# Shifted weight tiles for products of halves, and four leading tiles by ordinary products, in a two-layer hybrid network on Trainium2

## The chip, the cores and the metric

The kernel runs on one core of one Trainium2 chip. The metric is the device time of one execution in microseconds (us). The kernel before has a median of 2090.86 us over three runs (2090.5 to 2095.24). Engines go by short names: PE is TensorE, DVE VectorE, ACT ScalarE, POOL GpSimd, SP the engine that issues most DMAs.

## The reference, cut to what matters

Two layers run over a sequence of 512 tokens of width 1024. Each layer is a feed-forward block (FFN), a mixer block of three parallel mixers, and a second FFN. The change sits in the FFNs:

```python
def rmsnorm(x, g, eps=NORM_EPS):
    y = xf * lax.rsqrt(jnp.mean(xf * xf, axis=-1, keepdims=True) + eps)
    return y * g.astype(jnp.float32)

def swiglu(h, wg, wu, wd):
    return (jax.nn.silu(h @ wg) * (h @ wu)) @ wd

for i in range(DEPTH):                      # DEPTH = 2
    h = rmsnorm(x, ffn1_norm[i])
    x = x + MACARON_WEIGHT * swiglu(h, ffn1_wg[i], ffn1_wu[i], ffn1_wd[i])
    ...                                     # mixers
    h = rmsnorm(x, ffn2_norm[i])
    x = x + MACARON_WEIGHT * swiglu(h, ffn2_wg[i], ffn2_wu[i], ffn2_wd[i])
```

`wg` and `wu` are 1024 x 2816 (22 column tiles of 128), `wd` is 2816 x 1024. All is float32.

## The kernel before, in words

**Layout.** Activations lie transposed: 8 tiles of 128 channels x 512 tokens. Each float32 product is made of three products of a faster type (`float32r`): every operand is split into a high part (ACT copies it, rounded) and a low part (DVE subtracts), and PE adds high x high, high x low and low x high in a PSUM bank. Weights come from DRAM into `raw` (3 buffers), and their two parts go to `whi` and `wlo` (3 buffers each). `places()` allots all large tiles first, so that each starts at a multiple of 512 bytes.

**Ordinary products.** `gemm` (lines 269 to 287) makes a 128 x 512 output tile from 8 channel tiles: 3 x 8 = 24 matmuls of 512 columns, at lines 277, 285 and 286. `load_w` fetches and splits one weight tile (lines 262 and 263). `single` multiplies a gate tile and an up tile by the norm's factor (lines 521 and 522), applies silu, multiplies and splits the result.

**Products of halves.** Three of the four FFNs go through `ffn_halves`: the second of layer 0, and both of layer 1. It takes the 22 tile columns of `wg` and `wu` in pairs. For a pair `halves` makes, instead of 8 block products, 7 products of blocks of half the size (a scheme of Strassen and Winograd): `product` (lines 426 to 439) issues for each of them 3 x 4 = 12 matmuls of 256 columns at lines 436, 437 and 438, so one call of `halves` has 84 and one pair of tile columns, gate and up, has 168. Sums and differences of weight blocks are made by DVE (lines 462, 464, 479, 481) in `QG` and `ES`, and split like other weights (`split`, lines 290 and 291). Sums and differences of the activations, `T1` to `T4`, are made once for each FFN by `halves_of` (lines 407 to 423), four calls, each with two multiplications on ACT (line 415), three subtractions on DVE (419 to 421) and a split (290, 291) into `b0`, `b1`, `b2`, `b4`, `b5`, `b6` and `x`.

**Order.** `norm` first splits the 8 activation tiles without the norm's factor and lets PE begin at once; the factor `rstd` follows and is multiplied in when a PSUM bank is emptied. `gate(0)` makes the tile columns 0 and 1 by ordinary products (`firsts`: three weight tiles side by side in the three `mm` banks, the fourth in an `ms` bank) and then calls `halves_of`. `gate(1)` to `gate(10)` are pairs by halves. The down products (`down`, ordinary, into `ms` banks) come in groups behind the gates. A scheduler orders the instructions of each engine from the program's order and its own estimates; `behind` adds ordering constraints.

Of the kernel before, what the change touches and what calls it, by code (L numbers as in the profile page):

```python
# [8 lines left out]
F32 = mybir.dt.float32  # L9
F32R = mybir.dt.float32r  # L10
I32 = mybir.dt.int32
# [8 lines left out]
KD = D // 128  # L20
# [6 lines left out]

TAGS = {
    "x": (1024, 4), "hh": (512, 8), "hl": (512, 8),
    "raw": (1024, 3), "whi": (1024, 3), "wlo": (1024, 3),  # L30
    "rstd": (512, 1), "gain": (32, 2),
# [5 lines left out]
}  # L37
ORDER = ("x", "hh", "hl", "bk", "qr", "bh", "whi", "wlo", "b0", "b1", "b2", "b3", "b4", "b5", "b6", "QG", "ES", "yf",
         "bon", "g", "raw", "tm", "sg", "kk", "sq", "y", "w", "rstd", "kr")

# [68 lines left out]
def layout(z):  # L109
# [41 lines left out]
    def tiles(w):  # L151
# [3 lines left out]
    zz, xbc, dt, s, r = np.split(z["w_in"], [512, 1536, 1544, 1800], axis=2)  # L155
    t = lambda a, j: a[:, :, 128 * j:128 * j + 128]
    w_in = np.concatenate([s, t(r, 6), t(r, 2), t(r, 0), t(r, 4), t(r, 3), t(r, 1), t(r, 5)]
                          + [q for g in range(2) for q in (xbc[:, :, 256 * g:256 * g + 256], t(xbc, 4 + g),
                                                           t(xbc, 6 + g), zz[:, :, 256 * g:256 * g + 256])], 2)
    out = {  # L160
        "cst": constants(),
# [14 lines left out]
class Kernel:  # L176
# [5 lines left out]
    def places(self):  # L182

        start = self.sb.tile([128, 96], F32, tag="start", name="start", bufs=1)
        for tag in ORDER:
            n, bufs = TAGS[tag]
            assert n % 128 == 0
            self.sb.tile([128, n], F32, tag=tag, name=tag, bufs=bufs)

    def t(self, tag, shape, dt=F32):  # L190
        n, bufs = TAGS[tag]
        v = self.sb.tile([128, n], dt, tag=tag, name=tag, bufs=bufs)
        f = 1
        for s in shape[1:]:
            f *= s
        assert f <= n, (tag, shape)
        v = v[0:shape[0], 0:f]
        if len(shape) == 3:
            v = v.rearrange("p (a b) -> p a b", b=shape[2])
        elif len(shape) == 4:  # L200
            v = v.rearrange("p (a b c) -> p a b c", b=shape[2], c=shape[3])
        return v
# [238 lines left out]
    def halves(self, w, ops, out, n):  # L441

        nc = self.nc
        V = nc.vector
        H = L // 2
        raw = [self.fetch_w(w[m], KD, 128, [slice(0, KD)]) for m in range(2)]
        quarter = lambda m, k: raw[m].rearrange("p (q o) c -> p q o c", o=2)[:, :, k]
        hl = lambda shape: [self.t(t, shape, F32R) for t in ("whi", "wlo")]
        at = lambda w, o: [(lambda q, a=a: a[:, o, q]) for a in w]
        f = lambda a: a.rearrange("p s q c -> p (s q) c")  # L450
        snap = self.t(("bon", "g")[n % 2], [128, 4, H])
        keep = lambda j, r, by=1.0: nc.scalar.activation(out=snap[:, j], in_=r, func=AF.Copy, scale=by)

        w1 = hl([128, KD, 128])
        self.behind(self.split(raw[0], *w1), self.normed)
        w1 = [a.rearrange("p (q o) c -> p o q c", o=2) for a in w1]
        r1 = self.bank("mm", H)
        self.product(r1, at(w1, 0), ops, "B11", last=False)
        keep(0, r1)

        S = self.t(("QG", "ES")[n % 2], [128, 16, 128]).rearrange("p (s q) c -> p s q c", s=4)
        s1 = V.tensor_tensor(out=S[:, 0], in0=quarter(1, 0), in1=quarter(1, 1), op=ADD)
        self.behind(s1, self.normed)
        V.tensor_tensor(out=S[:, 1], in0=S[:, 0], in1=quarter(0, 0), op=SUB)
        w2 = hl([128, KD, 128])
        self.split(f(S[:, 0:2]), *w2)
        w2 = [a.rearrange("p (o q) c -> p o q c", o=2) for a in w2]
        r2 = self.bank("mr", H)
        self.product(r2, at(w1, 1), ops, "B21")
        V.tensor_tensor(out=out[:, 0, 0:H], in0=r2, in1=snap[:, 0], op=ADD)  # L470
        r3 = self.bank("mm", H)
        self.product(r3, at(w2, 0), ops, "T1", last=False)
        keep(3, r3)
        self.product(r1, at(w2, 1), ops, "T2", first=False, last=False)
        keep(1, r1)

        w4 = hl([128, KD // 2, 128])
        self.split(quarter(1, 1), *w4)
        s3 = V.tensor_tensor(out=S[:, 2], in0=quarter(0, 0), in1=quarter(1, 0), op=SUB)
        self.behind(s3, self.normed)  # L480
        V.tensor_tensor(out=S[:, 3], in0=quarter(0, 1), in1=S[:, 1], op=SUB)
        w3 = hl([128, KD, 128])
        self.split(f(S[:, 2:4]), *w3)
        w3 = [a.rearrange("p (o q) c -> p o q c", o=2) for a in w3]
        r4 = self.bank("mr", H)
        self.product(r4, [(lambda q, a=a: a[:, q]) for a in w4], ops, "T4")
        keep(2, r4, -1.0)
        self.product(r3, at(w3, 1), ops, "B22", first=False)
        V.tensor_tensor(out=out[:, 0, H:L], in0=r3, in1=snap[:, 1], op=ADD)
        self.product(r1, at(w3, 0), ops, "T3", first=False)  # L490
        V.tensor_tensor(out=out[:, 1], in0=r1.unsqueeze(1).to_broadcast([128, 2, H]), in1=snap[:, 2:4], op=ADD)

    def ffn_halves(self, gain, f, i, end=False):
        nc = self.nc
        wg, wu, wd = (self.a[f"{f}_{w}"][i] for w in ("wg", "wu", "wd"))
        act, rstd = self.norm(gain)
        slots = [self.t(n, [128, 2, 2 * L], F32R) for n in ("bk", "qr", "bh")]
        wide = rstd.unsqueeze(1).to_broadcast([128, 2, L])
        ops = []
# [7 lines left out]
        def firsts():  # L507

            w = lambda a, j: self.load_w(a[j], KD, 128)
            three = [(self.bank("mm"), w(*q)) for q in ((wg, 0), (wu, 0), (wg, 1))]  # L510
            self.gemms(three, act)
            ps = self.bank("ms")
            rest = w(wu, 1)
            single(0, three[0][0], three[1][0])
            self.gemm(ps, rest, act)
            single(1, three[2][0], ps)
# [13 lines left out]
        def gate(p):  # L530
            if p == 0:
                firsts()
                ops.extend(self.halves_of(act, gain, q) for q in range(KD // 2))
                return
            s, u = (self.t("p", [128, 2, L]) for _ in range(2))
            self.halves(wg[2 * p:2 * p + 2], ops, s, 0)
            nc.vector.tensor_tensor(out=s, in0=s, in1=wide, op=MUL)
            nc.scalar.activation(out=s, in_=s, func=AF.Silu)
            self.halves(wu[2 * p:2 * p + 2], ops, u, 1)
            nc.vector.tensor_tensor(out=u, in0=u, in1=wide, op=MUL)  # L540
            nc.vector.tensor_tensor(out=u, in0=u, in1=s, op=MUL)
            g = slots[p % 3]
            self.split(u, g[:, :, 0:L], g[:, :, L:2 * L])
            gs.extend((g[:, j, 0:L], g[:, j, L:2 * L]) for j in range(2))

        gs, left = [], []
        for n, (k0, nk) in enumerate(PAIRED):
# [5 lines left out]
            if end and first is None:  # L553
                ws = [self.load_w(wd[m, :, k0:k0 + nk], nk, 128, q)
                      for m, q in enumerate(("b0", "b1", "b2", "b4", "b5", "b6", "bon", "g"))]
                for h in range(2):
                    t = slice(256 * h, 256 * h + 256)
# [858 lines left out]
    def s5_tables(self, i):  # L1416

        nc = self.nc
        V, G = nc.vector, nc.gpsimd
        sp = self.small("s5p", [128, 4, 16])  # L1420
        self.dma(out=sp, in_=self.a["s5p"][i].rearrange("p (n g) -> p n g", n=4))
        sm = self.t("sg", [128, L])
        nxt = [128]
# [1 line left out]
        def t():  # L1425
            o = nxt[0]
            nxt[0] += 16
            return sm[:, o:o + 16]
# [1 line left out]
        pw = (lambda a: (a[:, 0], a[:, 1]))(self.t("g", [128, 2, L]))  # L1430
        v9 = lambda j: pw[j // 3][:, 144 * (j % 3):144 * (j % 3) + 144].rearrange("p (d g) -> p d g", g=16)
        PR, PI, SR, SI, NI, NR = (v9(j) for j in range(6))
        up = self.small("s5r", [128, 2, 8, 16])
        RR, RI = up[:, 0], up[:, 1]
        m1, m2 = (sm[:, 64 * j:64 * j + 64].rearrange("p (d g) -> p d g", g=16) for j in range(2))
        are, aim, ldt = (sp[:, j] for j in range(3))
        dt, mag, th, kq, co, si, w, w2 = (t() for _ in range(8))
        e1, e2, e3 = (t() for _ in range(3))
        ei = self.small("s5i", [128, 16], I32)
        self.exp_exact(ldt, dt, e1, e2, e3, ei)  # L1440
        V.tensor_tensor(out=w, in0=are, in1=dt, op=MUL)
        self.exp_exact(w, mag, e1, e2, e3, ei)
# [149 lines left out]
        G.memset(dT[:, :, 0:1], 0.0)  # L1592
        G.tensor_copy(out=dT[:, :, 1:], in_=mag.unsqueeze(2).to_broadcast([128, 16, 63]))
        self.s5 = halves, cT, sT, dT
        if i:
            self.s5_away(6, cT, sT, dT)
# [11 lines left out]
    def s5_again(self):  # L1608

        cut = [q for n in ("QG", "ES") for q in (lambda a: (a[:, 0:8], a[:, 8:16]))(self.t(n, [128, 16, 128]))]  # L1610
        cut += [self.t(n, [128, 8, 128]) for n in ("b0", "b1")]
        v = lambda q: q.rearrange("p g (d h) -> p g d h", h=16)
        halves = [(cut[n], v(cut[n + 1]), v(cut[n + 2])) for n in (0, 3)]
        self.s5 = halves, *(self.t(q, [128, 16, 64]) for q in ("b4", "b5", "b6"))
        halves, *rest = self.s5
        for n, q in enumerate(self.s5_flat((*halves[0], *halves[1], *rest))):
            self.nc.gpsimd.dma_start(out=q, in_=self.s5d[n])
# [187 lines left out]
```

## Time and profile before

| what | value |
|---|---|
| median of three runs | 2090.86 us |
| the profiled execution | 2088.86 us |
| span of its instructions | 2087.1 us |
| PE busy | 2002.3 us (96%), 16008 matmuls |
| DVE busy | 1578.0 us (76%) |
| ACT busy | 916.5 us (44%) |
| POOL busy | 361.0 us (17%) |
| mean granted PE clock | 0.983 of full speed |
| DMA | 200 MB, mean 96 GB/s |

The span is the time from the first to the last instruction of the one execution that was profiled; 1.8 us lie around it. That execution is 2.0 us under the median. PE busy is a sum of intervals that overlap (matmuls are pipelined), so the distance from the start of one matmul to the start of the next is the better measure of what one costs. The granted clock is either full (2.4 GHz) or half (1.2 GHz); a mean between tells how long each was granted.

### The profile page before, as it was taken

To read this page: it belongs to the slowest core of one execution; us is meant where nothing else is said; L and a number is where in the kernel's file an instruction comes from. 1 tells how busy PE (TensorE), PEld (TensorE's weight loads), DVE (VectorE), ACT (ScalarE), POOL (GpSimd) and SP (SyncE) were. 2 spreads that over 40 slices of the span, in tenths; PEclk is the share of its full clock that TensorE was granted. 3 is DMA by queue.
4 is the path that set the end of the run, shared out by engine and by line. 5 is a ranking of instruction groups with operands and counts; after the bars stand their busy time and mean duration, and the time that the engine had idled before them with its cause. 6 is when DMAs were issued, how large, how long until landed. Compare 5 with 4: busy or idle time off the path is not lost.

```text
span 2087.1 us, 39669 instructions
## 1 busy us (share of the span) xinstructions
PE 2002.3 (96%) x16008; PEld 1716.1 (82%) x16008; DVE 1578.0 (76%) x2570; ACT 916.5 (44%) x1404; POOL 361.0 (17%) x715
## 2 busy tenths in 40 slices
PE   8999999998999899999989999999899998999997
PEld 6788888776777699999969999987677777999996
DVE  6546555597569988877798888777956798888886
ACT  4222323443443645444464444444434445444443
POOL 0867656014121000000000000000222200000002
PEclk9999999999999999999999999999999999999998
DMA  4334332331202233333223333354111232333332
GB/s 158 113 117 137 112 112 82 125 122 33 61 12 77 84 101 96 107 112 102 75 96 102 92 103 105 110 191 150 51 54 35 60 96 66 106 101 102 91 103 80
DMA packets 89750, 200.00 MB, mean 96 GB/s; under 512 B 19040, under 2 KB 31328, under 8 KB 89568
## 3 DMA queue, kind: packets, MB, share of 16 engines
q1 hardware_dynamic: 82240, 186.85, 28.7%
q0 software_dynamic: 2592, 9.44, 1.2%
q8 instruction: 126, 2.06, 0.4%
q10 hardware_dynamic: 4736, 1.18, 0.3%
q14 instruction: 56, 0.46, 0.1%
HBM read 184.19 MB, written 12.06 MB: 94 GB/s over the span
## 4 chain that ended last, share of the span: by engine, by line
PE 79%; DVE 11%; issue 3%; ACT 2%; DMA 2%; POOL 1%; ACTq 0%; SPq 0%; POOLq 0%; DVEq 0%
PE mm L277 9%; PE mm L285 8%; PE mm L286 8%; PE mm L436 7%; PE mm L438 7%; PE mm L437 7%; PE ms L286 6%; PE ms L277 6%; PE ms L285 5%; PE mr L437 3%; PE mr L436 3%; PE mr L438 3%; DVE wlo L263 2%; PE mr L1039 1%; DMA raw<-in_ffn_wu 1%
## 5 line engine op out<-in xcount | busy, mean ns | idle before, releaser
L262 ACT ACTIVATE whi<-raw 128x512 fp32r<-128x512 f32 (+3 forms) x333 | 238.4, 718 | 476.2 <-PE mm L285 216.3
L277 PE MATMUL mm<-hh,whi 128*128 128x512 f32 x864 | 353.3, 412 | 18.3 <-ACT whi L262 14.2
L285 PE MATMUL mm<-hl,whi 128*128 128x512 f32 x864 | 341.4, 395 | 1.4 <-DVE hl L291 1.4
L286 PE MATMUL mm<-hh,wlo 128*128 128x512 f32 x864 | 342.3, 397 | 0.5 <-DVE wlo L263 0.5
L263 DVE TENSOR_TENSOR wlo<-raw,whi 128x512 fp32r<-128x512 f32 (+3 forms) x333 | 281.8, 848 | 58.8 <-ACT whi L262 58.0
L277 PEld LDWEIGHTS mm<-hh,whi 128*128 128x128 f32 x864 | 164.7, 191 | 60.3 <-ACT whi L262 18.8
L286 PEld LDWEIGHTS mm<-hh,wlo 128*128 128x128 f32 x864 | 163.8, 190 | 37.9 <-DVE wlo L263 1.8
L285 PEld LDWEIGHTS mm<-hl,whi 128*128 128x128 f32 x864 | 164.5, 190 | 32.9 <-DVE hl L291 2.5
L436 PE MATMUL mm<-b,whi 128*128 128x256 f32 x540 | 155.5, 288 | 24.4 <-ACT whi L290 24.4
L290 ACT ACTIVATE whi<-raw 128x1024 fp32r<-128x1024 f32 x120 | 101.5, 846 | 173.2 <-PE mm L437 104.6
L437 PE MATMUL mm<-b,whi 128*128 128x256 f32 x540 | 154.8, 287 | 0.0
L438 PE MATMUL mm<-b,wlo 128*128 128x256 f32 x540 | 154.8, 287 | 0.0
L438 PE MATMUL mm<-hh,wlo 128*128 128x256 f32 x480 | 135.9, 283 | 0.6 <-DVE wlo L291 0.6
L437 PE MATMUL mm<-hl,whi 128*128 128x256 f32 x480 | 135.1, 283 | 0.0
L436 PE MATMUL mm<-hh,whi 128*128 128x256 f32 x480 | 135.1, 283 | 0.0
L436 PEld LDWEIGHTS mm<-b,whi 128*128 128x128 f32 x540 | 105.9, 196 | 25.0 <-ACT whi L290 25.0
L291 DVE TENSOR_TENSOR wlo<-raw,whi 128x1024 fp32r<-128x1024 f32 x120 | 114.3, 952 | 5.1 <-ACT whi L290 4.5
L437 PEld LDWEIGHTS mm<-b,whi 128*128 128x128 f32 x540 | 105.9, 196 | 0.0
L438 PEld LDWEIGHTS mm<-b,wlo 128*128 128x128 f32 x540 | 105.6, 196 | 0.0
L436 PEld LDWEIGHTS mm<-hh,whi 128*128 128x128 f32 x480 | 91.9, 192 | 1.6
L438 PEld LDWEIGHTS mm<-hh,wlo 128*128 128x128 f32 x480 | 92.0, 192 | 1.2 <-DVE wlo L291 0.8
L437 PEld LDWEIGHTS mm<-hl,whi 128*128 128x128 f32 x480 | 91.9, 191 | 1.2
(653 smaller groups left out, 5152.6 us busy)
## 6 DMA issues: line engine op xcount, KB each, us to landing
raw<-in_ffn_wu SPq DMA_DIRECT2D x88, 512.0 KB, 3.7
raw<-in_ffn_wg SPq DMA_DIRECT2D x87, 512.0 KB, 3.7
raw<-in_ffn_wd SPq DMA_DIRECT2D x152, 256.0 KB, 2.6
raw<-in_w_in SPq DMA_DIRECT2D x42, 512.0 KB, 3.7
raw<-in_w_out SPq DMA_DIRECT2D x32, 128.0 KB, 2.3
raw<-in_w_out SPq DMA_DIRECT2D x16, 256.0 KB, 2.7
raw<-in_ffn_wd SPq DMA_DIRECT2D x16, 192.0 KB, 2.4
xd<-x SPq DMA_DIRECT2D x12, 256.0 KB, 4.3
```

The lines of the kernel that those rows point to most:

```text
L262: nc.scalar.activation(out=hi[:, q], in_=raw[:, q], func=AF.Copy)
L263: sub = nc.vector.tensor_tensor(out=lo[:, q], in0=raw[:, q], in1=hi[:, q].bitcast(F32), op=SUB)
L277: first = nc.tensor.matmul(out=ps, lhsT=hi[:, k], rhs=ah, start=(k == 0), stop=False)
L285: nc.tensor.matmul(out=ps, lhsT=hi[:, k], rhs=al, start=False, stop=False)
L286: mm = nc.tensor.matmul(out=ps, lhsT=lo[:, k], rhs=ah, start=False, stop=(k == last))
L290: self.nc.scalar.activation(out=hi, in_=src, func=AF.Copy)
L291: return self.nc.vector.tensor_tensor(out=lo, in0=src, in1=hi.bitcast(F32), op=SUB)
L436: nc.tensor.matmul(out=ps, lhsT=hi(q), rhs=ah, start=first and q == 0, stop=False, skip_group_check=True)
L437: nc.tensor.matmul(out=ps, lhsT=hi(q), rhs=al, start=False, stop=False, skip_group_check=True)
L438: nc.tensor.matmul(out=ps, lhsT=lo(q), rhs=ah, start=False, stop=last and q == len(ops) - 1, skip_group_check=True)
L1039: nc.tensor.matmul(out=b[s, j], lhsT=lh[s, j], rhs=rh[s, j], start=True, stop=True)
```

## The change

Three things are edited. The two weight tiles get 128 more elements, and in `halves` their data start 16 elements (64 bytes) into the tile, while the moving operands stay at multiples of 512 bytes (`SHIFT`, and the argument `o` of `t`); `load_w` and so all ordinary products keep weights at multiples of 512 bytes. `gate(1)` makes the tile columns 2 and 3 by four ordinary products, and two calls of `halves_of` stand behind each of the two gate-and-up pairs; `gate(0)` no longer calls it. The small tables of the S5 mixer (`s5p`, `s5r`, `s5i`) lie in tile `b3` in place of tiles of their own.

```diff
-    "raw": (1024, 3), "whi": (1024, 3), "wlo": (1024, 3),
+    "raw": (1024, 3), "whi": (1152, 3), "wlo": (1152, 3),
...
+SHIFT = 16
...
-    def t(self, tag, shape, dt=F32):
+    def t(self, tag, shape, dt=F32, o=0):
...
-        assert f <= n, (tag, shape)
-        v = v[0:shape[0], 0:f]
+        assert o + f <= n, (tag, shape)
+        v = v[0:shape[0], o:o + f]
...
-        hl = lambda shape: [self.t(t, shape, F32R) for t in ("whi", "wlo")]
+        hl = lambda shape: [self.t(t, shape, F32R, SHIFT) for t in ("whi", "wlo")]
...
         def gate(p):
             if p == 0:
                 firsts()
-                ops.extend(self.halves_of(act, gain, q) for q in range(KD // 2))
+                return
+            if p == 1:
+
+                for j in (2, 3):
+                    w = [self.load_w(a[j], KD, 128) for a in (wg, wu)]
+                    ps = [self.bank("mm") for _ in w]
+                    for q in zip(ps, w):
+                        self.gemm(*q, act)
+                    ops.extend(self.halves_of(act, gain, q) for q in (2 * j - 4, 2 * j - 3))
+                    single(j, *ps)
                 return
...
-        sp = self.small("s5p", [128, 4, 16])
+        own = self.t("b3", [128, 512])
+        sp = own[:, 0:64].rearrange("p (n g) -> p n g", n=4)
...
-        up = self.small("s5r", [128, 2, 8, 16])
+        up = own[:, 64:320].rearrange("p (n d g) -> p n d g", n=2, d=8)
...
-        ei = self.small("s5i", [128, 16], I32)
+        ei = own[:, 320:336].bitcast(I32)
```

Lines move by 2 up to `halves` (the products are at 438 to 440, `gemm` at 279, 287 and 288, the splits at 292 and 293) and by 11 or 12 behind `gate`.

The rows below are from the second FFN of layer 0; the two FFNs of layer 1 have the same pattern.

**PE, from the last ordinary product to the products of halves.** Names with a number are buffers: `mm_7405` is the bank of the first product of halves, `mm_7440` the first that needs the second weight tile `whi_7422` and the activation sums `b0`, `b1`. Before:

```order
L436 MATMUL mm_7405<-hh_7162,whi_7401 128x256
L437 MATMUL mm_7405<-hl_7163,whi_7401 128x256
L438 MATMUL mm_7405<-hh_7162,wlo_7402 128x256
L436 MATMUL mm_7440<-b0_7360,whi_7422 128x256
L437 MATMUL mm_7440<-b1_7361,whi_7422 128x256
L436 MATMUL mm_7405<-b0_7360,whi_7422 128x256
L437 MATMUL mm_7405<-b1_7361,whi_7422 128x256
L436 MATMUL mr_7477<-b0_7360,whi_7467 128x256
```

And changed, where `mm_7453` is the bank of the up product of tile column 3, and `mm_7541` of the first product of halves:

```order
L279 MATMUL mm_7453<-hh_7164,whi_7448 128x512
L287 MATMUL mm_7453<-hl_7165,whi_7448 128x512
L288 MATMUL mm_7453<-hh_7164,wlo_7449 128x512
L438 MATMUL mm_7541<-hh_7125,whi_7537 128x256
L439 MATMUL mm_7541<-hl_7126,whi_7537 128x256
L440 MATMUL mm_7541<-hh_7125,wlo_7538 128x256
L438 MATMUL mm_7541<-hh_7136,whi_7537 128x256
L439 MATMUL mm_7541<-hl_7137,whi_7537 128x256
```

The 24 matmuls of 512 columns of each of `mm_7362`, `mm_7363`, `mm_7452` and `mm_7453` now stand ahead of the first product of halves, and the 168 matmuls of 256 columns of the pair of tile columns 2 and 3 are gone.

**DVE, behind the last write of the norm (`sg`).** `mm` in the last row is the bank of the gate product of tile column 0. Before:

```order
L337 TENSOR_TENSOR sg<-cst,rrmry 128x512
L291 TENSOR_TENSOR wlo<-raw,whi 128x1024
L419 TENSOR_TENSOR QG<-QG 128x512
L419 TENSOR_TENSOR ES<-ES 128x512
L420 TENSOR_TENSOR QG<-QG 128x256
L521 TENSOR_TENSOR sq<-mm,rstd 128x512
```

And changed:

```order
L339 TENSOR_TENSOR sg<-cst,rrmry 128x512
L265 TENSOR_TENSOR wlo<-raw,whi 128x1024 x2
L421 TENSOR_TENSOR QG<-QG 128x512
L421 TENSOR_TENSOR ES<-ES 128x512
L523 TENSOR_TENSOR sq<-mm,rstd 128x512
```

One more weight tile is subtracted ahead of the emptying of the first `mm` bank, and one half-size subtraction less.

**DVE, up to the low part of the second weight tile of the first pair by halves (`wlo<-QG`).** Before:

```order
L291 TENSOR_TENSOR b_7381<-QG,b_7380 128x1024
L470 TENSOR_TENSOR p<-mr,bon 128x256
L291 TENSOR_TENSOR bk<-w,bk 128x512
L291 TENSOR_TENSOR x<-ES,x 128x1024
L462 TENSOR_TENSOR QG<-raw 128x512
L479 TENSOR_TENSOR QG<-raw 128x512
L291 TENSOR_TENSOR bk<-y,bk 128x512
L464 TENSOR_TENSOR QG<-QG,raw 128x512
L481 TENSOR_TENSOR QG<-raw,QG 128x512
L291 TENSOR_TENSOR wlo<-QG,whi 128x1024
```

And changed:

```order
L265 TENSOR_TENSOR wlo<-raw,whi 128x1024
L464 TENSOR_TENSOR QG<-raw 128x512
L481 TENSOR_TENSOR QG<-raw 128x512
L293 TENSOR_TENSOR x<-ES,x 128x1024
L466 TENSOR_TENSOR QG<-QG,raw 128x512
L524 TENSOR_TENSOR w<-mm,rstd 128x512
L293 TENSOR_TENSOR wlo<-raw,whi 128x1024
L483 TENSOR_TENSOR QG<-raw,QG 128x512
L526 TENSOR_TENSOR w<-w,sq 128x512
L523 TENSOR_TENSOR kk<-mm,rstd 128x512
L293 TENSOR_TENSOR qr<-w,qr 128x512
L293 TENSOR_TENSOR wlo<-QG,whi 128x1024
```

The chain that ends in `wlo<-QG` now has the emptying of the banks of tile columns 2 and 3 and their weights between its parts.

## Rows read from the trace of the kernel before

**Rows 1.** The page's part 1: span, and busy us of each engine.

```profile
span 2087.1 us, 39669 instructions
...
PE 2002.3 (96%) x16008; PEld 1716.1 (82%) x16008; DVE 1578.0 (76%) x2570; ACT 916.5 (44%) x1404; POOL 361.0 (17%) x715
```

**Rows 2.** What PE waited for, whole span: us in total, times, longest us.

```profile
PE mm L436 <- ACT whi L290: 24.4, 3, 8.1
```

**Rows 3.** PE timeline at the first such wait: start us, us, engine, line, operation.

```profile
721.25 0.28 PE L438 MATMUL mm<-hh,wlo 128*128 128x256 f32 x1
...
729.65 0.58 PE L436 MATMUL mm<-b,whi 128*128 128x256 f32 x1 [8.13 <-ACT whi L290]
```

**Rows 4.** PE timeline behind the second such wait; 9 starts apart.

```profile
1090.13 0.41 PE L438 MATMUL mm<-b,wlo 128*128 128x256 f32 x1
...
1092.05 0.41 PE L438 MATMUL mm<-x,wlo 128*128 128x256 f32 x1
```

**Rows 5.** Busy us by stretch: PE, PEld, DVE, ACT, POOL, then granted clock, DMA.

```profile
729.60:734.60 5.00, 4.95 (x25) 4.95 (x26) 4.47 (x6) 1.85 (x3) 0.00 (x0) 0.55 0.65 204
1088.60:1093.60 5.00, 4.92 (x27) 4.92 (x28) 4.42 (x6) 1.89 (x4) 0.00 (x0) 0.61 0.60 204
1746.60:1751.60 5.00, 4.93 (x24) 4.93 (x25) 4.54 (x6) 1.87 (x4) 0.00 (x0) 0.53 0.67 206
```

**Rows 6.** PE timeline, the last ordinary product of tile column 1.

```profile
718.50 0.39 PE L286 MATMUL ms<-hh,wlo 128*128 128x512 f32 x1
```

**Rows 7.** DVE timeline behind the norm.

```profile
715.54 1.22 DVE L291 TENSOR_TENSOR wlo<-raw,whi 128x1024 fp32r<-128x1024 f32 x1
...
717.88 0.42 DVE L420 TENSOR_TENSOR QG<-QG 128x256 f32<-128x256 f32 x1
...
718.21 0.69 DVE L521 TENSOR_TENSOR sq<-mm,rstd 128x512 f32<-128x512 f32 x1
```

**Rows 8.** ACT and DVE timeline, second weight tile of the first pair by halves.

```profile
728.54 1.06 ACT L290 ACTIVATE whi<-QG 128x1024 fp32r<-128x1024 f32 x1 [4.39 <-DVE QG L464]
...
729.63 1.23 DVE L291 TENSOR_TENSOR wlo<-QG,whi 128x1024 fp32r<-128x1024 f32 x1 [0.40 <-ACT whi L290]
```

**Rows 9.** PE timeline, products of halves in full flow; 12 starts apart.

```profile
1950.25 0.28 PE L436 MATMUL mm<-hh,whi 128*128 128x256 f32 x1
...
1951.69 0.28 PE L438 MATMUL mm<-b,wlo 128*128 128x256 f32 x1
```

**Rows 10.** PE timeline, ordinary products in full flow; 4 starts apart.

```profile
914.07 0.39 PE L286 MATMUL ms<-qr,wlo 128*128 128x512 f32 x1
...
914.98 0.39 PE L277 MATMUL ms<-bh,whi 128*128 128x512 f32 x1
```

**Rows 11.** PE timeline, first products of halves behind ordinary ones; 3 starts apart.

```profile
768.18 0.28 PE L436 MATMUL mm<-hh,whi 128*128 128x256 f32 x1
...
768.52 0.28 PE L436 MATMUL mm<-hh,whi 128*128 128x256 f32 x1
```

**Rows 12.** PE timeline, first ordinary products behind halves; 4 starts apart.

```profile
788.68 0.40 PE L277 MATMUL ms<-bk,whi 128*128 128x512 f32 x1
...
789.61 0.39 PE L285 MATMUL ms<-bk,whi 128*128 128x512 f32 x1
```

**Rows 13.** Line 436, first and last of six rows: duration ns, starts, forms.

```profile
L436 PE MATMUL mm<-b,whi x540: 282/283/584, 729.7 to 2032.5; 128*128 128x256 f32 x180
...
L436 PE MATMUL mr<-x,whi x60: 283/283/284, 735.7 to 2031.4; 128*128 128x256 f32 x60
```

**Rows 14.** Busy us by stretch in a stage of pairs by halves, columns as above.

```profile
800.00:900.00 100.00, 100.00 (x724) 95.04 (x724) 84.22 (x112) 49.02 (x75) 0.00 (x0) 1.00 0.32 96
```


## The prediction

> **What bounds the kernel now.** I read the page's part 1 first, then the list of what PE waited for, then PE's timeline at the longest wait, then the starts of matmuls in full flow. PE is busy nearly all of the span, every other engine far less [rows 1], so time goes only where PE waits, runs at half clock, or has fewer or cheaper matmuls. The reader is to see two things. One kind of wait stands out: three times 8.1 us, 24.4 us in all [rows 2], at the same place in each of the three FFNs by halves: the first product that needs the second weight tile. PE starts the matmul before it at 721.25 and this one at 729.65 [rows 3]; ACT's copy of that tile began at 728.54 and DVE's low part at 729.63 [rows 8], at the end of DVE's queue of work behind the norm. And behind each such wait PE runs at 1.2 GHz for a while: the granted clock of the 5 us from the restart is 0.55, 0.61 and 0.53 [rows 5], and matmuls of 256 columns start 1.92 / 9 = 0.213 us apart [rows 4], against 1.44 / 12 = 0.120 us in full flow [rows 9].
>
> **The waits (removed).** Between the last ordinary product of tile column 1 and the first product of halves PE now has four ordinary products, 4 x 24 = 96 matmuls. They start 0.91 / 4 = 0.2275 us apart [rows 10], so they give DVE 21.8 us. PE would then be ready for the second weight tile at 718.5 [rows 6] + 1.2 (a new wait, below) + 21.8 + 24 x 0.115 for the two products that need only the first weight tile = 744.3, on the time axis of the first FFN. DVE's chain ended at 729.65. New in it are four subtractions of weight tiles, the first of them in the place of one that was there, so 3 more, one for the first tile of halves, four emptyings of banks, two multiplications and two splits: 4 x 1.14 (1.22 us busy [rows 7], 1.14 from start to start) + 8 x 0.6 (0.69 busy [rows 7], 0.6 from start to start) = 9.4 us, so it ends near 739. DVE is some 5 us early where it was 8 us late. The wait goes: -24.4 us. With it goes the half clock: time at half clock in the three stretches is 2 x 5 x (1 - clock) = 4.5 + 3.9 + 4.7 = 13.1 us, of which 1 - 0.120 / 0.213 = 0.44 is lost: -5.7 us.
>
> **The tiles by ordinary products (added).** 168 x 0.120 = 20.2 us go, 96 x 0.2275 = 21.8 us come: +1.7 us in each FFN, +5.0 us.
>
> **A new short wait.** The gate product of tile column 2 takes the `mm` bank of tile column 0, which DVE empties behind one more weight tile (1.14) and without one half-size subtraction (0.33, busy 0.42 [rows 7]): its start moves from 718.21 to 719.0 and its end, 0.69 later, to 719.7. PE is free at 718.5 (the two matmuls of halves that stood ahead of the last ordinary ones stand behind them now). That is 1.2 us, +3.6 us in all. I take no loss of clock with it.
>
> **The shift.** 27 pairs are left by halves, 27 x 168 = 4536 matmuls (5040 before; line 436 has a third of them, in six groups of which the first and last are shown [rows 13]). In full flow one takes 0.120 us. At half clock one takes 0.213 us [rows 4], which leaves no fixed part beside 256 columns at 1.2 GHz; at full clock those columns take half of that, 0.1067 us, so 13.3 ns of each is something else. Ordinary products show the same: 0.2275 us, with 0.2133 for 512 columns. This part isn't constant. The first products of halves behind ordinary ones start 0.34 / 3 = 0.113 to 0.115 us apart (times are rounded to 0.01) with the same operands, tiles and clock [rows 11], and settle to 0.120 within a dozen; the first ordinary products behind halves start 0.93 / 4 = 0.2325 us apart [rows 12] and settle to 0.2275. So the cost depends on how two streams, the moving operand and the weights of the next matmul, stand to each other in time. The addresses modulo 512 are the one thing about these streams that is the same in every product of both sorts now, and the shift changes it for the products of halves alone. No row has such a matmul with another offset, so the price is bounded: -13.3 ns each (nothing left) and +7 ns each (in proportion to what the early ordinary ones of [rows 12] show above their best, 5 ns, and some more). I take 115 ns, the early value of [rows 11], since it is the nearest row: the same instruction in a different relation of the streams. 4536 x -5 ns = -22.7 us.
>
> The Trainium skill speaks against this term: "SBUF — State Buffer", section "Who interferes with whom", gives PE two independent read ports, one for the moving operand and one for weights, and says that PE never waits on anyone. By that the shift is worth nothing, and the sum would be 2069 us. The spread of [rows 11] against [rows 9] shows that something beside the columns varies, so I don't follow it, but it is a rival.
>
> **The S5 tables in `b3`.** They are written and read in the first FFN of layer 0, the next user of `b3` comes in the mixer; POOL, which reads them, is busy 17% of the span [rows 1]. If that cover were gone, a wait in the mixer of a few us would show; I take 0.
>
> **Sum.** -24.4 - 5.7 + 5.0 + 3.6 - 22.7 = -44.2 us. The profiled execution took 2088.86 us, 2.0 under the median of 2090.86; 2044.7 there, **2047 us** on the scale of the median.
>
> **Rivals.**
> 1. *The shift is worth nothing*; 0.120 us stays. For it: the fixed part is alike for 256 and 512 columns, which a constant cost of each matmul would be too. Against: it varies at one address. The time: 2047 + 22.7 = 2069 us.
> 2. *The shift removes most of the fixed part*: 0.1105 us, between the early 0.115 and the bare 0.1067. For it: if the streams meet once for each matmul, as one cost for each, whatever its length, suggests, a shift may move the meeting out of the moving operand's time. Against: no row is under 0.113. 4536 x -9.5 ns = -43 us: 2069 - 43 = 2026 us. DVE, at 84 of 100 us in such a stage [rows 14], would stand it. "TensorE: Matmul & The Clock Gate" of the Trainium skill, section "Back-to-back issue gap", has N / 2.4 + 2.5 ns, 109 ns here; by it, as an estimate, the sum would be near 2020 us, and the 120 ns of the trace disagree with it today.
> 3. *The shift puts the streams where they cost more, and the kernel is slower.* At +7 ns each, 4536 matmuls cost 31.8 us: 2069 + 32 = 2101 us. It decides from 21.5 us / 4536 = +4.7 ns, where the gain of the tiles is used up. For it: ordinary products show that both better and worse relations exist. Against: products of halves in full flow are at the top of what they show, not at the bottom.
> 4. *The wait stays in part.* DVE's chain ends later than reckoned (it waits for the bank of tile column 3, which PE fills late), so that PE loses 4 us and a stretch at half clock in each FFN: 3 x 4.1 + 5.7 = 18 us, 2065 us. Against: the 5 us in hand.
>
> **How the numbers follow.** Forecast (shift worth about 5 ns, wait gone) 0.40; rival 1 0.27; rival 2 0.20; rival 3 0.05; rival 4 0.08. The forecast's own range, 3 to 7 ns, is 2038 to 2056. The range of 8 in 10 takes in rivals 1, 2 and 4 with a few us on either side: 2018 to 2074 us. A measurement of this kernel can tell a change of about 0.3%, 6.3 us, from none. Under 2084.6 us lie the forecast and rivals 1, 2 and 4, less a little for a smaller loss by the shift: faster 0.92, same 0.03, slower 0.05.
>
> **What would show it.** The wait of the products' line for ACT's copy is gone from PE's list, and the clock stays full in the three stages; a wait near 1 us for DVE or for a bank's emptying stands at the first product of tile column 2. The starts of matmuls of 256 columns in full flow: 0.115 (forecast), 0.120 (rival 1), 0.110 (rival 2), 0.125 or more (rival 3); those of 512 columns stay at 0.2275. If matmuls of 512 columns change too, or a new wait for weights of halves is seen over 3 us, the reasoning is wrong at that term.

## The result and the profile after

The changed kernel takes **2060.3 us** (median of 4 runs, 2058.19 to 2061.9), the kernel before, measured with it, 2092.22 us (4 runs, 2090.5 to 2095.24): a ratio of 0.9845, interval 0.9828 to 0.9862, or 31.9 us less. The range of 2018 to 2074 us holds it; the forecast's own range, 2038 to 2056 us, misses it by 4 us. The profiled execution took 2058.19 us. Its page, part 1, against [rows 1]:

```profile
span 2056.1 us, 39153 instructions
PE 1991.3 (97%) x15792; PEld 1691.5 (82%) x15792; DVE 1546.5 (75%) x2528; ACT 900.0 (44%) x1374; POOL 357.0 (17%) x715
```

PE has 216 matmuls fewer (3 x 168 of halves gone, 3 x 96 ordinary ones added), and is still the engine that bounds the kernel.

What PE waited for, over the whole span (total us, times, longest):

```profile
PE mm L279 <- ACT whi L264: 17.1, 11, 6.0
PE mm L279 <- DVE up L696: 2.9, 2, 1.5
PE mm L279 <- DVE sq L523: 2.5, 3, 0.8
```

The 24.4 us of [rows 2] are gone from the list. The third row is the new short wait, for DVE's emptying of a bank (`sq`): 0.8 us of idle time each where the prediction had 1.2. The first two rows stand in ordinary products, took 16.8 and 2.9 us before as well, and are no part of the change.

The windows view of the three stages in which PE used to wait (the stretch and its length, busy time and count of PE, PEld, DVE, ACT and POOL, the granted clock, the DMA share and GB/s):

```profile
715.00:745.00 30.00, 29.12 (x138) 23.81 (x137) 27.67 (x41) 15.11 (x21) 0.00 (x0) 1.00 0.30 95
1062.00:1092.00 30.00, 29.08 (x139) 23.83 (x138) 27.21 (x40) 13.60 (x20) 0.65 (x2) 1.00 0.29 91
1710.00:1740.00 30.00, 29.12 (x136) 23.70 (x135) 28.10 (x44) 15.22 (x21) 0.00 (x0) 1.00 0.32 102
```

The clock is full in all three, where [rows 5] had 0.53 to 0.61; DVE is now busy for 27 to 28 of 30 us there.

PE's timeline in the first of these stages (start, duration, engine, line, operation, output and operands, sizes; in brackets a wait and who ended it):

```profile
719.26 0.39 PE L288 MATMUL ms<-hh,wlo 128*128 128x512 f32 x1
720.49 0.50 PE L279 MATMUL mm<-hh,whi 128*128 128x512 f32 x1 [0.83 <-DVE sq L523]
...
742.38 0.28 PE L438 MATMUL mm<-hh,whi 128*128 128x256 f32 x1
...
745.21 0.28 PE L438 MATMUL mm<-b,whi 128*128 128x256 f32 x1
```

And DVE's there:

```profile
737.14 0.69 DVE L523 TENSOR_TENSOR kk<-mm,rstd 128x512 f32<-128x512 f32 x1 [1.29 <-PE mm L288]
738.35 1.22 DVE L293 TENSOR_TENSOR wlo<-QG,whi 128x1024 fp32r<-128x1024 f32 x1
```

PE spends 720.49 to 742.38, 21.9 us, on the 96 added matmuls. The low part of the second weight tile of halves begins at 738.35 and ends at 738.35 + 1.22 = 739.6, and PE first wants that tile at 745.21: DVE is 5.6 us early where PE stood 8.1 us waiting in [rows 3]. The first row is the last matmul of tile column 1; it starts 0.76 us later here than in [rows 6], so that much has to be taken off to compare times of this stage with those of the trace before.

From 742.38 to 745.21 there are 24 starts, 0.118 us each, against the 0.120 us of [rows 9]. Over all products of halves the mean distance from one start to the next, pauses left out, was 119.9 ns before and is **117.5 ns** now; that of ordinary matmuls of 512 columns did not move (227.8 and 227.8). By the starts the shift is thus worth 4536 x 2.4 = 10.9 us.

### The profile page after: what moved, and what is told of

It reads as the page before. It is cut to its first block, busy times and chain, and to the rows that moved or that the text cites. A ratio compares the mean times of both kernels' runs of the same rounds, so it can differ in the third digit from the quotient of the medians.

```text
span 2056.1 us, 39153 instructions
## 1 busy us (share of the span) xinstructions
PE 1991.3 (97%) x15792; PEld 1691.5 (82%) x15792; DVE 1546.5 (75%) x2528; ACT 900.0 (44%) x1374; POOL 357.0 (17%) x715
## 4 chain that ended last, share of the span: by engine, by line
PE 81%; DVE 9%; issue 3%; ACT 2%; DMA 2%; POOL 1%; SPq 0%; POOLq 0%; DVEq 0%; ACTq 0%
PE mm L279 11%; PE mm L287 10%; PE mm L288 10%; PE mm L440 6%; PE mm L438 6%; PE mm L439 6%; PE ms L279 6%; PE ms L288 6%; PE ms L287 6%; PE mr L438 2%; PE mr L439 2%; PE mr L440 2%; DVE wlo L265 2%; PE mr L1050 1%; ACT whi L264 1%
## 5 line engine op out<-in xcount | busy, mean ns | idle before, releaser
L279 PE MATMUL mm<-hh,whi 128*128 128x512 f32 x960 | 390.6, 409 | 20.1 <-ACT whi L264 14.7
L288 PE MATMUL mm<-hh,wlo 128*128 128x512 f32 x960 | 379.5, 396 | 1.0 <-DVE wlo L265 1.0
L287 PE MATMUL mm<-hl,whi 128*128 128x512 f32 x960 | 378.8, 395 | 1.4 <-DVE hl L293 1.4
L265 DVE TENSOR_TENSOR wlo<-raw,whi 128x512 fp32r<-128x512 f32 (+3 forms) x345 | 299.0, 870 | 55.9 <-ACT whi L264 55.4
L438 PE MATMUL mm<-b,whi 128*128 128x256 f32 x486 | 136.4, 281 | 0.0
L440 PE MATMUL mm<-b,wlo 128*128 128x256 f32 x486 | 136.4, 281 | 0.0
L439 PE MATMUL mm<-b,whi 128*128 128x256 f32 x486 | 136.4, 281 | 0.0
L440 PE MATMUL mm<-hh,wlo 128*128 128x256 f32 x432 | 121.2, 281 | 0.7 <-DVE wlo L293 0.7
L438 PE MATMUL mm<-hh,whi 128*128 128x256 f32 x432 | 120.6, 280 | 0.0
L439 PE MATMUL mm<-hl,whi 128*128 128x256 f32 x432 | 120.5, 280 | 0.0
L293 DVE TENSOR_TENSOR wlo<-raw,whi 128x1024 fp32r<-128x1024 f32 x108 | 102.7, 951 | 12.9 <-ACT whi L292 12.2
L438 PEld LDWEIGHTS mm<-b,whi 128*128 128x128 f32 x486 | 92.0, 189 | 0.1
L439 PEld LDWEIGHTS mm<-b,whi 128*128 128x128 f32 x486 | 91.7, 189 | 0.1
```

The source lines that it names most:

```text
L265: sub = nc.vector.tensor_tensor(out=lo[:, q], in0=raw[:, q], in1=hi[:, q].bitcast(F32), op=SUB)
L279: first = nc.tensor.matmul(out=ps, lhsT=hi[:, k], rhs=ah, start=(k == 0), stop=False)
L287: nc.tensor.matmul(out=ps, lhsT=hi[:, k], rhs=al, start=False, stop=False)
L288: mm = nc.tensor.matmul(out=ps, lhsT=lo[:, k], rhs=ah, start=False, stop=(k == last))
L293: return self.nc.vector.tensor_tensor(out=lo, in0=src, in1=hi.bitcast(F32), op=SUB)
L438: nc.tensor.matmul(out=ps, lhsT=hi(q), rhs=ah, start=first and q == 0, stop=False, skip_group_check=True)
```

## The experiments

**1. The tiles without the shift (e1_no_shift).**

```diff
-SHIFT = 16
+SHIFT = 0
```

> The changed kernel with the weights of the products of halves back at multiples of 512 bytes (SHIFT = 0). Theory A (the tiles and the shift each gave their own part, and the shift gave what the starts show: 119.9 ns before, 117.5 ns after, times 4536 matmuls = 11 us): matmuls of 256 columns start 0.120 us apart again and the kernel takes about 2060 + 11 = 2071 us. Rival B (the shift is worth nothing; the shorter distance comes from the new order of the work): 0.1175 us stays, 2060 us. Rival C (the shift is worth the 22.7 us that were forecast and something else was lost): about 2083 us.

Measured: 2072.55 us (5 runs, 2071.39 to 2076.83), ratio 0.9906, interval 0.9892 to 0.992, or 20.4 us less than before. PE's timeline, two matmuls of 256 columns 24 starts apart, again 0.1200 us each:

```profile
746.68 0.28 PE L440 MATMUL mm<-hh,wlo 128*128 128x256 f32 x1
...
749.56 0.28 PE L440 MATMUL mm<-b,wlo 128*128 128x256 f32 x1
```

The tiles, the removed waits and the clock bring 20.4 us; the shift is worth the other 2072.55 - 2060.3 = 12.2 us, and the distance is at 120 ns as soon as the weights lie at multiples of 512 bytes. That rival 1, a shift worth nothing, is wrong is shown here. A pause doesn't change the distance at this offset: behind two of 0.50 and 0.18 us in the midst of long runs it is 120.0 ns as before them.

**2. The shift without the tiles (e2_shift_only).** The gate stage of before, the weights 64 bytes on:

```diff
             if p == 0:
                 firsts()
-                return
-            if p == 1:
...
+                ops.extend(self.halves_of(act, gain, q) for q in range(KD // 2))
                 return
```

> The changed kernel with the gate of before: tile columns 2 and 3 by halves, the shift kept. Theory A: the three waits of 8.1 us and the half clock behind them are back, 5040 matmuls at 0.1175 in place of 0.120: 2092 - 12 = about 2080 us. Rival B: 2092 us. If the waits were not the tiles' doing, they would be absent here too, and the time near 2050 us.

Measured: 2074.54 us (6 runs, 2069.89 to 2082.55), ratio 0.9925, interval 0.9907 to 0.9943: 18.4 us less than before, and more than the 12 that were expected. The list of waits has the old one back, at its old size:

```profile
PE mm L438 <- ACT whi L292: 24.3, 3, 8.1
```

So the wait went through the changed gate stage and not through the shift. The four tiles and the later place of `halves_of`, which come with it, were not taken apart. The surprise is in PE's timeline, behind the stretch at half clock that follows the wait:

```profile
734.80 0.28 PE L438 MATMUL mr<-b,whi 128*128 128x256 f32 x1
...
737.52 0.28 PE L439 MATMUL mr<-hl,whi 128*128 128x256 f32 x1
```

24 starts in 2.72 us, 0.1133 us each, at the same addresses that gave 0.118 in the changed kernel. The first long run of products of halves stays at 113 ns in two of the three FFNs and at 118 in the third. Three more long runs begin at 118 and go over to 113 within ten matmuls of a mere hitch without idle time, in which one start comes 24 to 38 ns late and the next another 0.1 us, as here (the last two rows are again 24 starts apart, 0.1133 us each):

```profile
990.60 0.28 PE L439 MATMUL mm<-hl,whi 128*128 128x256 f32 x1
990.75 0.39 PE L440 MATMUL mm<-hh,wlo 128*128 128x256 f32 x1
990.97 0.28 PE L438 MATMUL mm<-hh,whi 128*128 128x256 f32 x1
...
995.41 0.28 PE L438 MATMUL mr<-hh,whi 128*128 128x256 f32 x1
...
998.13 0.28 PE L439 MATMUL mm<-b,whi 128*128 128x256 f32 x1
```

Not every pause does it: behind an idle time of 0.24 us in another run 118 stays. The mean over all 5040 is 116.65, and 5040 x 3.2 = 16 us. The execution with this trace is the fastest of the six, 19 us under the profiled one of before; no trace shows how the slower ones were divided between the two distances. One offset has two steady distances, then; the later experiments ask what chooses between them.

**3. Offsets of 0 to 448 bytes in one kernel (e3_offsets_by_64).** Each pair of tile columns gets its own offset:

```diff
-        hl = lambda shape: [self.t(t, shape, F32R, SHIFT) for t in ("whi", "wlo")]
+        hl = lambda shape: [self.t(t, shape, F32R, self.shift) for t in ("whi", "wlo")]
...
+            self.shift = 16 * (p - 2)
```

> The changed kernel with another offset of the weights for each pair by halves: pairs 2 to 10 of each feed-forward block have offsets of 0, 64, 128, ... 512 bytes modulo 512. Theory A (the cost depends on the offset modulo 512): the distance of starts is 0.120 us in pairs 2 and 10 (offset 0 and 512) and 0.1175 in pair 3; the others show the curve, somewhere between 0.113 and 0.126. Rival B: the same distance in all pairs. Rival D (any offset from 0 gives the same gain, what matters is not to be at the same address): 0.120 in pairs 2 and 10 and 0.1175 in all others.

Measured (one run): 2067.06 us. The mean distance of starts by the offset of the weights, worked out from all starts of the trace:

| bytes | 0 | 64 | 128 | 192 | 256 | 320 | 384 | 448 |
|---|---|---|---|---|---|---|---|---|
| ns | 119.8 | 117.4 | 118.6 | 117.8 | 119.8 | 117.5 | 118.6 | 117.8 |

Three of them as PE's timeline has them, each over 24 starts: 0 bytes (0.1200 us), 128 (0.1188) and 256 (0.1200):

```profile
744.34 0.28 PE L440 MATMUL mm<-hh,wlo 128*128 128x256 f32 x1
...
747.22 0.28 PE L440 MATMUL mm<-b,wlo 128*128 128x256 f32 x1
...
807.11 0.28 PE L438 MATMUL mm<-hh,whi 128*128 128x256 f32 x1
...
809.96 0.28 PE L440 MATMUL mm<-x,wlo 128*128 128x256 f32 x1
...
868.47 0.28 PE L439 MATMUL mm<-hl,whi 128*128 128x256 f32 x1
...
871.35 0.28 PE L438 MATMUL mm<-x,whi 128*128 128x256 f32 x1
```

The second half of the table repeats the first: the cost has a period of 256 bytes, not 512, and no offset does better than 64 bytes does in the mean.

**4. Offsets of 16 to 128 bytes (e4_offsets_by_16).**

```diff
-            self.shift = 16 * (p - 2)
+            self.shift = 4 * (p - 2)
```

> Offsets of 0, 16, 32, ... 128 bytes for pairs 2 to 10. By 64 bytes the first study gave 119.8, 117.4, 118.6 and 117.8 ns at 0, 64, 128 and 192 and the same again from 256. Theory A (the meeting of the two streams moves with the offset): a smooth curve with its least value somewhere between 16 and 112 bytes, perhaps under 117 ns. Rival F (64-byte steps are what counts): 120 ns at 0 to 48, 117.5 from 64 to 112, 118.6 at 128.

Measured (one run): 2062.48 us; mean distances by offset:

| bytes | 0 | 16 | 32 | 48 | 64 | 80 | 96 | 112 | 128 |
|---|---|---|---|---|---|---|---|---|---|
| ns | 119.8 | 118.3 | 118.3 | 118.2 | 116.2 | 118.6 | 118.6 | 119.9 | 118.6 |

This is neither a smooth curve nor steps of 64 bytes: 16 bytes already give 1.5 ns, and 112 bytes nothing. Both theories missed. The 116.2 at 64 bytes is a mixture of stretches at 113 (in one FFN) and at 118 (in two), as in experiment 2.

**5. The ordinary products' weights moved (e5_ordinary_offsets).** The weight tiles that `load_w` makes lie, eight after eight, 64 bytes further on than the eight before, 0 to 448:

```diff
+            self.loads += 1
+            o = 16 * (self.loads // 8 % 8)
-            hi, lo = (self.t(n, [128, k, m], F32R) for n in ("whi", "wlo"))
+            hi, lo = (self.t(n, [128, k, m], F32R, o) for n in ("whi", "wlo"))
```

> The changed kernel in which the weights of ordinary products lie at offsets of 0, 64, ... 448 bytes, another one for every 8 weight tiles; the halves stay at 64. Theory A: the distance of starts of 512 columns, 0.227 us at offset 0, depends on the offset too, with a spread of 2 to 8 ns; an offset that is better than 0 would be worth up to 5000 x 2 ns = 10 us. Rival E (with twice the columns for each weight tile the two streams have room, and only their start matters): 0.227 at every offset.

Measured (one run): 2066.13 us, 6 us more than the changed kernel. Mean distance of matmuls of 512 columns:

| bytes | 0 | 64 | 128 | 192 | 256 | 320 | 384 | 448 |
|---|---|---|---|---|---|---|---|---|
| ns | 228.0 | 233.3 | 232.4 | 230.0 | 227.6 | 233.3 | 232.3 | 229.3 |

PE's timeline, two pairs of matmuls nine starts apart, offset 0 (2.04 / 9 = 0.227 us) and 64 (2.10 / 9 = 0.233):

```profile
15.28 0.39 PE L291 MATMUL mm<-hh,wlo 128*128 128x512 f32 x1
...
17.32 0.39 PE L282 MATMUL mm<-hh,whi 128*128 128x512 f32 x1
...
694.74 0.39 PE L290 MATMUL mm<-hl,whi 128*128 128x512 f32 x1
...
696.84 0.39 PE L290 MATMUL mm<-hl,whi 128*128 128x512 f32 x1
```

The period is 256 bytes again, and the preference is turned round: for 512 columns 64 bytes is the dearest and 0 or 256 the cheapest. The second finding is that the products of halves, all still at 64 bytes, fell to a mean of 115.6 ns. Whole runs of them went at 113.3 ns and others at 117.8, and a run mostly kept what it began with. By the last down tile ahead of it, a run of 320 began at 113 behind 64 or 320 bytes (3 of 3), behind 128 (2 of 2) and behind 448 (1 of 1), and at 118 behind 0, 192, 256 or 384 (6 of 6); the run of 156 behind the up tile of column 3 began at 113 behind 128 or 384 and at 118 behind 64. So the ordinary products ahead of a run seem to choose its distance; the next experiments test it.

**6. Two tiles as a push, 128 bytes (e6_kick_128).** If so, it is enough to move the last ordinary weight tile ahead of each run: the up tile of column 3, and the last down tile of each group (`o` is a new argument of `load_w`, which `down` passes on).

```diff
+KICK = 32
...
-            hi, lo = (self.t(n, [128, k, m], F32R) for n in ("whi", "wlo"))
+            hi, lo = (self.t(n, [128, k, m], F32R, o) for n in ("whi", "wlo"))
...
+                    w = [self.load_w(a[j], KD, 128, o=KICK if j == 3 and a is wu else 0) for a in (wg, wu)]
...
+            o = KICK if m == KD - 1 else 0
```

> The changed kernel, in which the last ordinary weight tile ahead of each run of products of halves (the last down tile of a group, the last up tile of column 3) lies at an offset of 128 bytes. In the study of ordinary offsets runs of halves that followed ordinary products at this offset went at 0.1133 us a matmul throughout, others at 0.1178, and a run kept what it began with. Theory G (there are two steady distances, and the beginning of a run chooses): most runs go at 0.1133, 4000 matmuls gain 4.4 ns: about 2060 - 17 = 2043 us. Rival H (the distances of that study came from its other differences): 0.1178 stays, 2060 us.

Measured: 2057.96 us (4 runs, 2055.25 to 2061.55), ratio 0.983, interval 0.9807 to 0.9852, which overlaps that of the changed kernel. PE's timeline, 24 starts each, behind the up tile (0.1133 us) and behind the down tiles (0.1175):

```profile
743.28 0.28 PE L440 MATMUL mm<-hl,whi 128*128 128x256 f32 x1
...
746.00 0.28 PE L440 MATMUL mm<-b,whi 128*128 128x256 f32 x1
...
787.02 0.28 PE L440 MATMUL mm<-b,whi 128*128 128x256 f32 x1
...
789.84 0.28 PE L441 MATMUL mm<-x,wlo 128*128 128x256 f32 x1
```

Half a miss: the push works behind the up tile, in all three runs of 156 matmuls, and not behind the down tiles, where the twelve runs of 320 all begin at 117.8 (two of them go over to 113.3 behind a pause). In experiment 5 both runs behind a last down tile at 128 bytes began at 113. There the down tile before it lay at 128 or 64 bytes, here at 0: the last tile does not decide alone.

**7. The same push with 448 bytes (e7_kick_448).**

```diff
-KICK = 32
+KICK = 112
```

> The same with 448 bytes, of which that study has one run, at 0.1133 us. Theory G: about 2043 us if that run was no accident, 2060 if it was. Rival H: 2060 us.

Measured: 2065.12 us (4 runs, 2061.9 to 2066.41), ratio 0.9866, interval 0.9846 to 0.9886; the mean distance is 117.3 ns and no long run began at 113. A miss: ahead of the one run behind 448 bytes in experiment 5 the down tile before the last lay at 384 bytes, here it lies at 0.

**8. Each push with the offset that worked at its place (e10_kick_two).** The up tile of column 3 at 128 bytes as in experiment 6, the last down tile of a group at 64 as in experiment 5. Against experiment 6:

```diff
-            o = KICK if m == KD - 1 else 0
+            o = SHIFT if m == KD - 1 else 0
```

> The changed kernel; the last up tile of column 3 lies at 128 bytes, as in the run with that offset, where the runs of halves behind it went at 0.1133 us each of three times; the last down tile of a group lies at 64 bytes, since in the study of ordinary offsets all three runs of halves behind down tiles at 64 or 320 bytes (the same modulo 256) went at 0.1133. Theory G (the exit from the ordinary products chooses between two steady distances): nearly all of 4536 matmuls at 0.1133 in place of 0.1175, about 2060 - 18 = 2042 us, down to 2045 with the cost of the offset in those tiles. If the choice is chance, a mixture as in the earlier runs, 2055 to 2062 us.

Measured: **2048.23 us** (5 runs, 2046.97 to 2054.22), ratio 0.9798, interval 0.9777 to 0.9819, which lies below that of the changed kernel (from 0.9828): this version is faster than the changed kernel too. PE's timeline, 24 starts, now behind the down tiles too at 0.1133 us:

```profile
784.01 0.28 PE L439 MATMUL mr<-hh,whi 128*128 128x256 f32 x1
...
786.73 0.28 PE L440 MATMUL mm<-b,whi 128*128 128x256 f32 x1
```

All 15 long runs begin at 113.3 ns. The mean is 114.0, not 113.3, since in 6 of the 12 runs of 320 the last 90 matmuls or so fall back to 117.8; why was not tried. 4536 x (117.5 - 114.0) = 15.9 us, less 264 ordinary matmuls that the push makes 5 to 6 ns dearer (1.5 us), is 14.4; measured are 12 us by the two medians, and 10 by the two ratios, each against runs of the kernel before made beside it. The expected 2042 to 2045 us had nearly all 4536 matmuls at 113.3.

## Why the prediction was right, and where a term was off

**The waits: right.** The wait is gone in all three FFNs, and rival 4 with it; experiment 2 brings it back at 8.1 us with the gate stage of before. "PE would be ready at 744.3" came out at 745.21, or 744.45 on the time axis of before. One reading in this term was wrong: 729.65, at which "DVE's chain ended", is where PE starts again, behind ACT's copy; DVE's low part begins at 729.63 there and ends at 730.86 [rows 8]. So "near 739" forecasts the beginning of the low part, which came at 738.35, or 737.6 on the axis of before, 1.5 us earlier. The margin was large enough for both. What rival 4 feared is there, but small: DVE waits 1.29 us for the bank of tile column 3.

**The clock and the added tiles: right.** The clock is full in the three stages; the 96 added matmuls took 21.9 us for 21.8. **The new short wait** stands where it was put. Its 1.2 us were reckoned from the start of the last matmul of tile column 1, and from there PE's next start came 720.49 - 719.26 = 1.23 us later; 0.23 of that is the ordinary distance, so 1.0 us is lost, and the list shows 0.8 as idle. **The S5 tables** were put at 0: the three largest waits of PE in the mixers are 6.7, 3.7 and 2.3 us in all, where before they were 6.0, 3.6 and 2.4; no run moves the tables alone. Experiment 1 measures these four terms together, with the shift taken out: -20.4 us, for -24.4 - 5.7 + 5.0 + 3.6 = -21.5. By that run's interval it is -16.7 to -22.6 us, so the sum holds within the noise.

**The shift: right in its sign, and half its size.** The step that failed is "I take 115 ns, the early value of [rows 11], since it is the nearest row". It measured 117.5 ns, and 12.2 us by experiment 1 in place of 22.7. The inference ahead of it held as far as it says that the part of a matmul beside its columns is not constant and moves with the address of the weights; that the relation of two streams is behind it is not shown. What failed was to read a value out of the first three matmuls behind a change of stage as the steady value at another address. [rows 11] shows distances just after ordinary products; a run then settles. At 64 bytes there are two distances on which it can settle, 113.3 and 117.8 ns, and in the changed kernel all 15 long runs come out of ordinary products onto the dearer one, which one of them leaves midway; the runs of 12 that stand between down products go at 113.8. Experiments 6 and 8 show that the tiles ahead of a run can choose, by changing nothing but the last of them. So the total of 2060.3 us lies nearer to rival 1's 2069 than to the forecast's 2047, and the range of 8 in 10 holds it because it was drawn around both: that speaks for the breadth of the range, not for the 115 ns.

**The rivals.** Rival 1 falls with experiment 1. The rule of the Trainium skill that went with it ("SBUF — State Buffer", section "Who interferes with whom": PE never waits on anyone) is not borne out here as far as it would exclude an effect of addresses: with nothing else edited, PE's mean distance is 119.9 ns at offset 0 and 117.5 at 64. Rival 2's 110.5 ns was reached by no run; the lowest steady distance is 113.3. The 109 ns that go with N / 2.4 + 2.5 in the Trainium skill ("TensorE: Matmul & The Clock Gate", section "Back-to-back issue gap") were not reached either; the section gives this as the gap of an isolated matmul and says that in a stream of weight loads and matmuls both set the spacing, and every matmul here has a weight load of its own. Rival 3's mechanism, an offset that costs more, exists, but for the ordinary products (experiment 5: 233.3 ns at 64 bytes for 228.0 at 0), which this change leaves at multiples of 512 bytes.

**The sum** was -44.2 us for -31.9: of the 12 us between, 22.7 - 12.2 = 10.5 are the shift's, and about 1 is that of the four other terms.

**What stays open:** what inside PE or its memory makes the cost. The runs show only that the offset of the weights, with a period of 256 bytes, the number of columns and the matmuls ahead matter. Offsets of the moving operand were not tried, so whether the weights' own address counts or its relation to the moving operand is not shown. Nor is it shown which late start or which of the tiles ahead brings a run to 113.3 ns, and which not.

## What to carry to other kernels

A wait that ends a whole queue of work on another engine is removed by giving the waiting engine other work that is ready; count the chain of the late engine instruction by instruction and compare its end with the new need, which here came out within 1.5 us. Where the same instruction shows two distances in one trace, don't price an edit by the better one: look first at whether it holds for hundreds of instructions or only for the first few behind a change of stage. In a kernel bound by matmuls with a weight load each, the address of the weights is worth trying for each width of matmul by itself, and so are the addresses of the tiles just ahead of a long run.

## What the runs showed that was not expected

- The cost of a matmul depends on the offset of its weights with a period of 256 bytes, and oppositely for 256 columns (0 bytes dearest, 119.8 ns; 64 bytes 117.4) and for 512 (0 bytes cheapest, 228.0; 64 bytes 233.3).
- A stream of like matmuls has two steady distances with its weights at 64 bytes, 113.3 and 117.8 ns, and mostly keeps for 150 to 300 matmuls the one on which it began. In the changed kernel one run went over from 117.8 to 113 behind a pause of 0.66 us; in experiment 2 a hitch of 0.13 us without idle time was enough.
- Moving one up tile by 128 bytes and the last down tile of each group by 64 brings 10 to 12 us of 2060 (experiment 8).
